# Modulation vectors of two FFN stages: from TensorE matmuls to VectorE products with a sum along the row

## The chip, the cores and the metric

One NeuronCore of a Trainium2 chip runs the whole program. The metric is the device time of one execution in microseconds; for the kernel before there are three timed executions and one more under the hardware profiler.

The engines are named as in the profile: PE is TensorE, DVE VectorE, ACT ScalarE, POOL GpSimd, SP SyncE (here it only issues DMAs).

## The reference, cut to what matters

Two diffusion-transformer blocks follow each other on a latent sequence of 512 tokens and a context of 256 tokens, model width 1024. The first block has two layers (layers 0 and 1 below), the second has one (layer 2). Every layer takes its shifts, scales and gates from an adaLN modulation: the condition vector through SiLU, times a 1024 x 6144 matrix, plus a bias. This is done for two conditions, the latent's and the context's.

```python
def adaln(cond, w_mod, b_mod):
    m = jnp.dot(jax.nn.silu(cond), w_mod) + b_mod
    return jnp.split(m[..., None, :], 6, axis=-1)

sh1, sc1, g1, sh2, sc2, g2 = adaln(c, w_mod[l], b_mod[l])
csh1, csc1, cg1, csh2, csc2, cg2 = adaln(c_ctx, w_mod[l], b_mod[l])
...
x = x + g1 * jnp.einsum('blm,md->bld', mix, w_out[l])
x = x + g2 * swiglu(modulate(rms_norm(x, norm2_g[l]), sh2, sc2), w_ffn_in[l], w_ffn_out[l])
```

## The kernel before

**Arithmetic.** Every large product is computed in three fp32r matmuls: weight and activation are each split into a rounded high part and a rest (`whi`/`wlo`, `hh`/`hl`), and high x high, low x high and high x low are summed in PSUM (`mm3`, L255, L258, L259). The splitting of weights is done on the chip, in `Weights._load`: SP loads half a weight tile (512 KB) into a tile `raw` (L226), ACT casts it into `whi` in two pieces (L229), POOL subtracts to get `wlo` (L231). The split tiles have two buffers, `raw` has four.

**Modulation.** The three layers' modulation is cut into 72 slots of 256 columns, (l, s) in the list `mods`. A slot's weights (1 MB, two `raw` tiles, L218) come from the same four `raw` buffers as the other weights, but are not split. `mod_slot` (L335 to L365) multiplies them in plain fp32 on TensorE: eight calls of a 32 x 256 result (L344; 16 instructions in the trace), the k chunks spread over the four row groups of one PSUM tile. ACT copies that to `ev` (L350), two transposes put columns on partitions (L355), DVE adds the four row groups (`TENSOR_REDUCE`, L357), adds the bias (L359), and for scale slots applies the norm's gain (L363).

**Where the slots run.** `mod_fill` takes slots off the list. 28 of them run at the start and in the mixing stages, where the code puts them between other work. The other 44 are called by `ffn`, one in each step j of layers 0 and 1 (`mod_fill` at L961, 22 steps each). The first four of them are layer 0's own FFN gate, which its first down projection reads (L895); the others are read in layers 1 and 2.

**The FFN.** In `ffn` a step j takes 128 hidden columns: 16 matmul positions of `mm3` over gate and up halves for the latent (tile `s2t`, 512 columns) and, in layer 0 only, as many for the context (`pj`, 256 columns). Then ACT takes SiLU of the gate (`sg`, L955), DVE multiplies by the up half out of PSUM (L956), ACT and POOL split the result (`gh` L327, `gl` L328). After a group of steps (four in layer 0, eight in layer 1, shorter ones at the end) the down projection reads the group's `gh`/`gl`; DVE adds its results into `xt` (`flush`, L895).

**Before the FFN** stands the output projection (`out_proj`), whose last halves run interleaved with the norm of the first halves: DVE and ACT apply it (`u` L423, `hh` L426, `hl` L431 on DVE or L429 on POOL), the row's root goes DVE `rsv` (L297), POOL `rsy` (L298), and a PE broadcast (L323).

**Order.** The program is written in Python order and a list scheduler fixes each engine's static instruction order before the run. Each engine runs its own list in order; semaphores hold an instruction until its inputs have been written and its output buffer is free. Also SP's DMA issues are one such list.

Of the kernel before, what the change touches and what calls it, by code (L numbers as in the profile page):

```python
# [18 lines left out]
D = 1024  # L19
# [20 lines left out]
def _ktile(w):  # L40
    k, n = w.shape
    return np.ascontiguousarray(w.reshape(k // 128, 128, n).transpose(1, 0, 2)).reshape(128, -1)
# [64 lines left out]
    }  # L107


def layout(inp):  # L110
    a = {k: np.asarray(v) for k, v in inp.items()}
    kc = _shape_constants()
    o = {}
# [3 lines left out]
    pv = {  # L117
        "c": a["c"], "c_ctx": a["c_ctx"], "c_2": a["c_2"], "c_ctx_2": a["c_ctx_2"],
        "b_mod0": a["b_mod"][0], "b_mod1": a["b_mod"][1], "b_mod2": a["b_mod_2"][0],
        "n1g0": a["norm1_g"][0], "n1g1": a["norm1_g"][1], "n1g2": a["g_norm_mix_2"][0],  # L120
        "n2g0": a["norm2_g"][0], "n2g1": a["norm2_g"][1], "n2g2": a["g_norm_ffn_2"][0],
        "ghn": a["g_hgrn_norm_2"][0], "gq": a["g_q_norm_2"][0], "gkv": a["g_kv_norm_2"][0],
        "lbf": a["lb_fwd_2"], "lbb": a["lb_bwd_2"], "gfin": a["g_final_2"],
    }
# [20 lines left out]
        o[n] = kc[n]  # L145
    wm = [a["w_mod"][0], a["w_mod"][1], a["w_mod_2"][0]]
    for l in range(3):
        o[f"w_mod{l}"] = np.stack([_ktile(wm[l][:, s * 256:(s + 1) * 256]) for s in range(24)])
    pw = np.zeros((2, 128, 2, 128), np.float32)
    for l in range(2):  # L150
        for ct in range(2):
# [91 lines left out]
class K:  # L243
# [87 lines left out]
    def cond(self, *names):  # L331
        for i, n in enumerate(names):
            self.nc.scalar.activation(out=self.cond_t[:, :, i], in_=self.pv(n), func=AF.Silu)

    def mod_slot(self, l, s, tag="pj"):  # L335

        nc = self.nc
        if (l, s) == (2, 0):
            self.cond("c_2", "c_ctx_2")
        raw = [r.rearrange("p (k n) -> p k n", k=4) for r in self.WM.next(("mod", l, s))]  # L340
        ps = self.ps([128, 256], tag)
        for k in range(KD):
            g = 32 * (k % 4)
            nc.tensor.matmul(ps[g:g + 32], lhsT=self.cond_t[:, k, :], rhs=raw[k // 4][:, k % 4, :],  # L344
                             start=k < 4, stop=k >= 4, tile_position=(0, g))

        ev = self.tmp("ev", [128, 256])

        def post():
            nc.scalar.copy(out=ev, in_=ps)  # L350

        def post2():
            pt = self.ps([128, 2, 128], tag)
            for i in range(2):
# [3 lines left out]
            bc = lambda ap: ap.unsqueeze(2).to_broadcast([128, 2, 2])
            nc.vector.tensor_tensor(out=m, in0=m, in1=bc(self.pv(f"b_mod{l}", 2 * s, 2)), op=ALU.add)  # L359
            q = s // 4  # L360
            if q in (1, 4):
                g = bc(self.pv(f"n{1 if q == 1 else 2}g{l}", 2 * (s % 4), 2))
                nc.vector.scalar_tensor_tensor(out=m, in0=m, scalar=1.0, in1=g, op0=ALU.add, op1=ALU.mult)  # L363
# [1199 lines left out]
    def run(self):  # L1563
# [22 lines left out]
        self.GS = [con.tile([128, 1], F32, name=f"gs{l}") for l in range(2)]  # L1586
        self.cond("c", "c_ctx")
        self.W = Weights(self, self.plan())
        self.mods = [(l, s) for l in range(3) for s in (0, 4, 1, 5, 2, 6, 3, 7) + tuple(range(8, 24))]
        self.WM = Weights(self, [(("mod", l, s), "mod", I[f"w_mod{l}"][s], 2048) for l, s in self.mods])  # L1590
        xs = [[p_dram.tile([128, KD * 256], F32, name=f"xs{l}{i}") for i in range(2)] for l in range(2)]
        v3 = lambda ap: ap.rearrange("p (k n) -> p k n", k=KD)
# [49 lines left out]
        with self.pool("u0") as self.p_u:  # L1642
            h2c, h2 = self.new_h("c"), self.new_h("x")
            self.out_proj(0, self.out_weights(0, 2, 3), hm, hmc, xt, xc, norms(0, 2, xt, h2, xc, h2c))
            self.hc, self.hx = self.new_h("c"), self.new_h("x")
            with self.pool("f0", bufs=8) as pf:
                self.ffn(0, pf, h2, h2c, xt, xc, norms(1, 1, xt, self.hx, xc, self.hc))
            store_xt(xs[0], xt)
        xpool.close()
# [4 lines left out]
        with self.pool("u1") as self.p_u:  # L1654
            h2 = self.new_h("x")
            self.out_proj(1, self.out_weights(1, 2, 3), hm, None, xt, None, norms(1, 2, xt, h2))
            self.hc, self.hx = self.new_h("c"), self.new_h("x")
            with self.pool("f1", bufs=13) as pf:
                xc2 = self.load_x(pf, "xc2", v3(I["c2T"]), NCX, 1)
                self.ffn(1, pf, h2, None, xt, None, norms(2, 1, xt, self.hx), {13: lambda: self.norm_mod(2, 1, xc2, 1, self.hc)})  # L1660
            store_xt(xs[1], xt)
# [99 lines left out]
```

## Time and profile before

| | |
|---|---|
| median of three runs | 2635.28 us (2625.0 to 2635.9) |
| profiled execution | 2631.17 us |
| its span in the trace | 2629.3 us |
| TensorE busy | 2488.1 us, 95% |
| VectorE busy | 966.3 us, 37% |
| ScalarE busy | 909.7 us, 35% |
| GpSimd busy | 1138.1 us, 43% |
| mean granted TensorE clock | 0.971 |

The span runs from the first to the last instruction in the trace; the execution's own time is 1.9 us longer. A busy share is an average over all stages; the stages that this change touches are the two FFNs, from about 450 to 1005 us and from about 1380 to 1770 us.

### The profile page before, as it was taken

To read this page: it belongs to the slowest core of one execution; us is meant where nothing else is said; L and a number is where in the kernel's file an instruction comes from. 1 tells how busy PE (TensorE), PEld (TensorE's weight loads), DVE (VectorE), ACT (ScalarE), POOL (GpSimd) and SP (SyncE) were. 2 spreads that over 40 slices of the span, in tenths; PEclk is the share of its full clock that TensorE was granted. 3 is DMA by queue.
4 is the path that set the end of the run, shared out by engine and by line. 5 is a ranking of instruction groups with operands and counts; after the bars stand their busy time and mean duration, and the time that the engine had idled before them with its cause. 6 is when DMAs were issued, how large, how long until landed. Compare 5 with 4: busy or idle time off the path is not lost.

```text
span 2629.3 us, 38620 instructions
## 1 busy us (share of the span) xinstructions
PE 2488.1 (95%) x15840; PEld 2121.3 (81%) x15840; DVE 966.3 (37%) x1897; ACT 909.7 (35%) x1909; POOL 1138.1 (43%) x960
## 2 busy tenths in 40 slices
PE   7889889999999999989999999999998899999998
PEld 5778779888888889877788777778887788888887
DVE  4897564122121114497542102123322756210113
ACT  4334444312112114333534223234443543422222
POOL 4655305333334335545326445444323354555553
PEclk9889989999999999989999999999998899999999
DMA  7113311323223233122324444343101021232221
GB/s 255 49 50 121 119 57 49 113 96 111 93 86 120 89 97 113 53 64 81 97 81 148 157 129 161 128 153 105 49 33 51 16 97 49 81 96 96 92 91 59
DMA packets 68978, 248.55 MB, mean 95 GB/s; under 512 B 7489, under 2 KB 10817, under 8 KB 67137
## 3 DMA queue, kind: packets, MB, share of 16 engines
q1 hardware_dynamic: 65568, 232.29, 27.1%
q10 hardware_dynamic: 3232, 13.79, 1.4%
q8 instruction: 125, 2.05, 0.3%
q14 instruction: 53, 0.43, 0.1%
HBM read 239.75 MB, written 6.29 MB: 94 GB/s over the span
## 4 chain that ended last, share of the span: by engine, by line
PE 48%; DVE 5%; ACT 2%; POOL 2%; DMA 1%; issue 1%; POOLq 0%; ACTq 0%; DVEq 0%; SPq 0%
PE s2t L255 6%; PE s2t L258 6%; PE s2t L259 6%; PE pj L255 5%; PE pj L258 5%; PE pj L259 5%; PE ap L820 2%; PE ap L259 1%; PE ap L258 1%; PE ap L255 1%; PE s2t L1533 1%; PE s2t L837 1%; DVE mix L665 1%; POOL wlo L231 1%; PE ap L344 1%; PE ap L816 1%
## 5 line engine op out<-in xcount | busy, mean ns | idle before, releaser
L231 POOL TENSOR_TENSOR wlo<-raw,whi 128x512 fp32r<-128x512 f32 x564 | 734.4, 1332 | 683.1 <-ACT whi L229 682.9
L229 ACT CAST whi<-raw 128x512 fp32r<-128x512 f32 x576 | 319.9, 616 | 681.5 <-PE pj L258 252.6
L258 PE MATMUL s2t<-hl,whi 128*128 128x512 f32 (+1 forms) x1184 | 445.6, 377 | 2.6 <-POOL hl L429 2.6
L255 PE MATMUL s2t<-hh,whi 128*128 128x512 f32 (+1 forms) x1184 | 446.9, 379 | 0.9 <-ACT whi L229 0.9
L259 PE MATMUL s2t<-hh,wlo 128*128 128x512 f32 (+1 forms) x1184 | 446.1, 377 | 0.0
L255 PE MATMUL pj<-hh,whi 128*128 128x256 f32 (+1 forms) x1088 | 337.3, 312 | 7.6 <-DVE mod L357 3.0
L258 PE MATMUL pj<-hl,whi 128*128 128x256 f32 (+1 forms) x1088 | 331.2, 305 | 3.3 <-DVE hl L431 2.3
L259 PE MATMUL pj<-hh,wlo 128*128 128x256 f32 (+1 forms) x1088 | 330.6, 305 | 0.0
L956 DVE TENSOR_TENSOR sg<-sg,s2t 128x512 f32<-128x512 f32 x66 | 45.4, 688 | 623.8 <-ACT sg L955 623.8
L258 PEld LDWEIGHTS s2t<-hl,whi 128*128 128x128 f32 x1184 | 222.7, 188 | 46.9 <-POOL hl L429 3.5
L255 PEld LDWEIGHTS s2t<-hh,whi 128*128 128x128 f32 x1184 | 222.3, 188 | 46.7 <-issue 1.6
L259 PEld LDWEIGHTS s2t<-hh,wlo 128*128 128x128 f32 x1184 | 222.7, 188 | 45.5 <-issue 0.8
L255 PEld LDWEIGHTS pj<-hh,whi 128*128 128x128 f32 x1088 | 211.0, 194 | 25.1 <-DVE mod L357 3.3
L328 POOL TENSOR_TENSOR gl<-sg,gh 128x512 fp32r<-128x512 f32 (+1 forms) x66 | 97.2, 1472 | 300.8 <-ACT gh L327 300.8
L258 PEld LDWEIGHTS pj<-hl,whi 128*128 128x128 f32 x1088 | 210.8, 194 | 12.5 <-DVE hl L431 2.5
L259 PEld LDWEIGHTS pj<-hh,wlo 128*128 128x128 f32 x1088 | 210.2, 193 | 8.7 <-issue 0.8
L255 PE MATMUL pj<-whi,hh 128*128 128x256 f32 x672 | 196.8, 293 | 2.5 <-ACT ev L350 1.3
L258 PE MATMUL pj<-wlo,hh 128*128 128x256 f32 x672 | 196.1, 292 | 0.0
L259 PE MATMUL pj<-whi,hl 128*128 128x256 f32 x672 | 194.9, 290 | 0.0
L895 DVE SCALAR_TENSOR_TENSOR xt<-pj,mod,xt 128x256 f32<-128x256 f32 x224 | 101.6, 480 | 174.4 <-PE pj L259 174.2
L955 ACT ACTIVATE sg<-s2t 128x512 f32<-128x512 f32 x66 | 39.2, 594 | 306.4 <-PE s2t L259 306.4
L259 PE MATMUL pj<-gh,wlo 128*128 128x512 f32 (+1 forms) x400 | 145.2, 363 | 0.0
(385 smaller groups left out, 4581.0 us busy)
## 6 DMA issues: line engine op xcount, KB each, us to landing
raw<-in_w_mod SPq DMA_DIRECT2D x144, 512.0 KB, 4.0
raw<-in_w_up SPq DMA_DIRECT2D x132, 512.0 KB, 4.0
raw<-in_w_dn SPq DMA_DIRECT2D x66, 512.0 KB, 3.9
raw<-in_w_in SPq DMA_DIRECT2D x60, 512.0 KB, 3.9
raw<-in_w_out SPq DMA_DIRECT2D x24, 512.0 KB, 3.8
xt<-xs ACTq DMA_DIRECT2D x4, 1024.0 KB, 4.9
xt<-in_xT ACTq DMA_DIRECT2D x2, 1024.0 KB, 8.8
xs<-xt SPq DMA_DIRECT2D x2, 1024.0 KB, 3.8
```

Of the source, the lines that this page charges most:

```text
L229: nc.scalar.copy(out=h, in_=raw[:, q])
L231: eng.tensor_tensor(out=lo[:, s][:, q], in0=raw[:, q], in1=h.bitcast(F32), op=ALU.subtract)
L255: i = mm(ps, lhsT=lh, rhs=rh, start=start, stop=False)
L258: mm(ps, lhsT=lh, rhs=rl, start=False, stop=False)
L259: return mm(ps, lhsT=ll, rhs=rh, start=False, stop=stop)
L328: (lo_eng or self.nc.vector).tensor_tensor(out=lo, in0=src, in1=hi.bitcast(F32), op=ALU.subtract)
L344: nc.tensor.matmul(ps[g:g + 32], lhsT=self.cond_t[:, k, :], rhs=raw[k // 4][:, k % 4, :], start=k < 4, stop=k >= 4, tile_position=(0, g))
L665: nc.vector.scalar_tensor_tensor(out=m, in0=u[:, j:j + W], scalar=dw(j), in1=m, op0=ALU.mult, op1=ALU.add)
L820: i = nc.tensor.matmul(o, lhsT=at[:, j], rhs=v[:, j0 + j, :], start=j0 + j == 0, stop=j0 + j == nj - 1)
L895: self.nc.vector.scalar_tensor_tensor(out=x, in0=ps, scalar=col, in1=x, op0=ALU.mult, op1=ALU.add)
L955: nc.scalar.activation(out=sg[:, c], in_=p[:, 0], func=AF.Silu)
L956: nc.vector.tensor_tensor(out=sg[:, c], in0=sg[:, c], in1=p[:, 1], op=ALU.mult)
```

## The change

For the 44 slots of the first two FFNs (`MODS[20:42]` and `MODS[50:72]`) the host lays the weights out transposed: a partition holds one modulation column, with its 1024 weights along the row; a slot is two such tiles of 128 columns. The function `cond_rows`, called once ahead of each of these FFNs, loads both condition vectors repeated on all partitions (1 MB, `cr`) and applies SiLU on ACT. `mod_rows` takes the place of the matmuls: for each of the two tiles and each of the two conditions, one DVE instruction multiplies the tile by the condition row and writes the row's sum through `accum_out`. The products themselves go to a tile `mjunk`, and for the second condition in place over `raw`. `mod_bias` adds the bias and applies the gain as before. To make room, the FFN pools have 6 buffers where they had 8 (layer 0) and 10 where they had 13 (layer 1). The other 28 slots stay as they were.

```diff
+def _nrows(w):
+
+    return np.ascontiguousarray(w.T.reshape(2, 128, D).transpose(1, 0, 2).reshape(128, 2 * D))
...
+MODS_ROWS = set(MODS[20:42] + MODS[50:72])
...
+    def cond_rows(self, pool, n):
+
+        self.CR = pool.tile([128, 2, D], F32, name="cr", bufs=1)
+        self.junk = pool.tile([128, D], F32, name="mjunk", bufs=1)
+        self.nc.scalar.dma_start(out=self.CR.rearrange("p c k -> p (c k)"), in_=self.I["cr"][n])
+        for i in range(2):
+            self.nc.scalar.activation(out=self.CR[:, i], in_=self.CR[:, i], func=AF.Silu)
+
+    def mod_rows(self, l, s):
+
+        nc = self.nc
+        raw = self.WM.next(("mod", l, s))
+        m = self.MOD[l][:, 2 * s:2 * s + 2, :]
+        acc = self.p_small.tile([128, 2, 2], F32, tag="macc", name="macc", bufs=2)
+
+        def part(i):
+            for ci in range(2):
+                nc.vector.scalar_tensor_tensor(out=raw[i] if ci else self.junk, in0=raw[i], scalar=1.0, in1=self.CR[:, ci],
+                                               op0=ALU.mult, op1=ALU.mult, accum_out=acc[:, i, ci:ci + 1])
+
+        return [(0, lambda: part(0)), (1, lambda: part(1)), (0, lambda: self.mod_bias(l, s, m, acc))]
...
     def mod_slot(self, l, s, tag="pj"):
 
         nc = self.nc
+        if (l, s) in MODS_ROWS:
+            return self.mod_rows(l, s)
...
-            with self.pool("f0", bufs=8) as pf:
+            with self.pool("f0", bufs=6) as pf:
+                self.cond_rows(pf, 0)
                 self.ffn(0, pf, h2, h2c, xt, xc, norms(1, 1, xt, self.hx, xc, self.hc))
...
-            with self.pool("f1", bufs=13) as pf:
+            with self.pool("f1", bufs=10) as pf:
+                self.cond_rows(pf, 1)
```

The change moves instructions at three places that matter below. Line numbers shift with it: L956 becomes L997, L359 L373, L363 L377, L218 L231, L226 L239, L297 L310, L431 L472; the new products are L365.

**VectorE in the middle of FFN 1.** `sg` is the gate product of a step, `mod_88` the modulation of layer 2, `PV` the biases and gains, `macc` the new row sums. Before, two steps in a row:

```order
L956 TENSOR_TENSOR sg<-sg,s2t 128x512 [waits Activation_49]
L357 TENSOR_REDUCE mod_88<-ap 128x4 [waits PE_49]
L359 TENSOR_TENSOR mod_88<-mod_88,PV 128x4 [waits DVE_49]
L956 TENSOR_TENSOR sg<-sg,s2t 128x512 [waits Activation_49]
L357 TENSOR_REDUCE mod_88<-ap 128x4 [waits PE_49]
L359 TENSOR_TENSOR mod_88<-mod_88,PV 128x4 [waits DVE_49]
L363 SCALAR_TENSOR_TENSOR mod_88<-mod_88,PV 128x4 [waits DVE_49]
```

With the change, one step:

```order
L997 TENSOR_TENSOR sg<-sg,s2t 128x512 [waits Activation_49]
L365 SCALAR_TENSOR_TENSOR mjunk,macc<-raw,cr 128x1024 [waits DMAHW3_49]
L365 SCALAR_TENSOR_TENSOR raw,macc<-raw,cr 128x1024 [waits DMAHW5_49,DVE_49,Pool_49]
L365 SCALAR_TENSOR_TENSOR mjunk,macc<-raw,cr 128x1024 [waits DMAHW4_49]
L365 SCALAR_TENSOR_TENSOR raw,macc<-raw,cr 128x1024 [waits DMAHW6_49,DVE_49,Pool_49]
L373 TENSOR_TENSOR mod_88<-macc,PV 128x4 [waits DVE_49]
L997 TENSOR_TENSOR sg<-sg,s2t 128x512 [waits Activation_49]
```

The reduce over PE's result is gone, and between two gate products stand four long products that wait for the slot's weights (a DMA) and for nothing of PE. In the first group of eight steps the products run two slots ahead of the steps, and between the last two gate products of that group there is none.

**SyncE's DMA issues in FFN 1.** Weights of the up projection (`in_w_up`) and of the modulation (`in_w_mod`) take turns in the four `raw` buffers. Before:

```order
L226 DMA raw<-in_w_up 128x1024 [waits DMAHW1_49,PE_49]
L226 DMA raw<-in_w_up 128x1024 [waits DMAHW2_49,PE_49]
L218 DMA raw<-in_w_mod 128x1024 [waits DMAHW7_49,Pool_49]
L218 DMA raw<-in_w_mod 128x1024 [waits DMAHW0_49,Pool_49]
L226 DMA raw<-in_w_up 128x1024 [waits DMAHW5_49,PE_49]
L226 DMA raw<-in_w_up 128x1024 [waits DMAHW6_49,PE_49]
```

With the change:

```order
L239 DMA raw<-in_w_up 128x1024 [waits DVE_49] x2
L231 DMA raw<-in_w_mod 128x1024 [waits DMAHW1_49,Pool_49]
L231 DMA raw<-in_w_mod 128x1024 [waits DMAHW2_49,Pool_49]
L239 DMA raw<-in_w_up 128x1024 [waits DVE_49] x2
L231 DMA raw<-in_w_mod 128x1024 [waits DMAHW5_49,DMAHW3_49,Pool_49]
```

The order of the loads is the same; the up weights' buffers are now given free by VectorE's products, where TensorE's slot gave them free before.

**VectorE at the start of FFN 0.** `u` and `hl` apply the norm to the first latent half (`xt_3680`) and then to the second (`xt_3682`), and `rsv` begins the second half's root. Before:

```order
L423 SCALAR_TENSOR_TENSOR u<-xt_3680,mod_86,ap 128x256 [waits DVE_49]
L431 SCALAR_TENSOR_TENSOR hl<-u,mod_86,hh 128x256 [waits Activation_49] x2
L297 TENSOR_SCALAR rsv<-ap 128x1 [waits PE_49] x2
L956 TENSOR_TENSOR sg<-sg,pj 128x256 [waits Activation_49]
L423 SCALAR_TENSOR_TENSOR u<-xt_3682,mod_86,ap 128x256 [waits DVE_49,PE_49]
```

With the change:

```order
L464 SCALAR_TENSOR_TENSOR u<-xt_3680,mod_86,ap 128x256 [waits DVE_49]
L365 SCALAR_TENSOR_TENSOR mjunk,macc<-raw,cr 128x1024 [waits DMAHW3_49]
L472 SCALAR_TENSOR_TENSOR hl<-u,mod_86,hh 128x256 [waits Activation_49]
L365 SCALAR_TENSOR_TENSOR raw,macc<-raw,cr 128x1024 [waits DMAHW7_49,DVE_49,Pool_49]
L472 SCALAR_TENSOR_TENSOR hl<-u,mod_86,hh 128x256 [waits Activation_49]
L310 TENSOR_SCALAR rsv<-ap 128x1 [waits PE_49]
L365 SCALAR_TENSOR_TENSOR mjunk,macc<-raw,cr 128x1024 [waits DMAHW4_49]
L310 TENSOR_SCALAR rsv<-ap 128x1 [waits PE_49]
L365 SCALAR_TENSOR_TENSOR raw,macc<-raw,cr 128x1024 [waits DMAHW0_49,DMAHW6_49,DVE_49,Pool_49]
L373 TENSOR_TENSOR mod_86<-macc,PV 128x4 [waits DVE_49]
L997 TENSOR_TENSOR sg<-sg,pj 128x256 [waits Activation_49]
```

Three products, two of which wait for a DMA of their own, now stand ahead of the second `rsv`.

## Rows read from the trace of the kernel before

**Rows 1.** The page, parts 1 and 2: busy time of TensorE, and its granted clock.
```profile
PE 2488.1 (95%) x15840; PEld 2121.3 (81%) x15840; DVE 966.3 (37%) x1897; ACT 909.7 (35%) x1909; POOL 1138.1 (43%) x960
...
PEclk9889989999999999989999999999998899999999
```

**Rows 2.** Windows view, the two FFNs: length, engines, granted clock, DMA share, GB/s.
```profile
413.00:1010.00 597.00, 596.05 (x3828) 513.98 (x3828) 122.04 (x279) 145.34 (x282) 223.29 (x178) 1.00 0.30 98
1340.00:1770.00 430.00, 422.27 (x2337) 337.73 (x2335) 83.23 (x189) 138.88 (x271) 219.10 (x183) 1.00 0.43 140
```

**Rows 3.** Timeline of TensorE around one slot in FFN 1 (start us, us, engine, instruction).
```profile
1447.77 0.39 PE L258 MATMUL s2t<-hl,whi 128*128 128x512 f32 x1
1448.00 0.40 PE L259 MATMUL s2t<-hh,wlo 128*128 128x512 f32 x1
1448.33 1.07 PE L344 MATMUL ap<-raw,cond 128*32 128x256 f32 x16
1449.33 0.44 PE L355 MATMUL ap<-ident,ev 128*128 128x128 f32 x2
...
1449.84 0.40 PE L258 MATMUL s2t<-hl,whi 128*128 128x512 f32 x1
```

**Rows 4.** Timeline of VectorE: the gate products of two following steps, FFN 0, FFN 1.
```profile
506.60 0.69 DVE L956 TENSOR_TENSOR sg<-sg,s2t 128x512 f32<-128x512 f32 x1 [10.93 <-ACT sg L955]
...
524.87 0.69 DVE L956 TENSOR_TENSOR sg<-sg,s2t 128x512 f32<-128x512 f32 x1 [10.93 <-ACT sg L955]
...
1461.70 0.69 DVE L956 TENSOR_TENSOR sg<-sg,s2t 128x512 f32<-128x512 f32 x1 [11.32 <-ACT sg L955]
...
1474.27 0.69 DVE L956 TENSOR_TENSOR sg<-sg,s2t 128x512 f32<-128x512 f32 x1 [11.52 <-ACT sg L955]
```

**Rows 5.** Source view, VectorE's products and a scan; ScalarE's group of accumulator reads.
```profile
L423 DVE SCALAR_TENSOR_TENSOR u<-xt,mod,ap x80: 466/476/482, 445.0 to 2253.8; 128x256 f32<-128x256 f32 x80
...
L665 DVE SCALAR_TENSOR_TENSOR mix<-uc,DWH,mix x120: 722/1020/2107, 79.8 to 1200.2; 128x783 f32<-128x783 f32 x60, 128x512 f32<-128x512 f32 x60
...
L845 DVE SCALAR_TENSOR_TENSOR e<-e,rr x40: 458/1010/1462, 127.8 to 1325.8; 128x768 f32<-128x768 f32 x32, 128x256 f32<-128x256 f32 x8
...
L1249 DVE TENSOR_TENSOR_SCAN b<-rst,sig x4: 1757/1758/1759, 2033.4 to 2149.2; 128x768 f32<-128x768 f32 x4
...
L804 ACT ACTIVATION_READ_ACCUMULATOR e<-s2t,nmx 128x1 f32 x96 | 19.2, 200 | 0.0
```

**Rows 6.** Timelines of VectorE and GpSimd in the mixing stage, both busy.
```profile
142.50 3.18 DVE L665 SCALAR_TENSOR_TENSOR mix<-uc,DWH,mix 128x783 f32<-128x783 f32 x2
...
145.68 1.97 DVE L665 SCALAR_TENSOR_TENSOR mix<-uc,DWH,mix 128x783 f32<-128x783 f32 x1
...
139.60 7.21 POOL L231 TENSOR_TENSOR wlo<-raw,whi 128x512 fp32r<-128x512 f32 x4 [12.67 <-ACT whi L229]
```

**Rows 7.** Timelines of FFN 1, one step: ScalarE, GpSimd, TensorE.
```profile
1467.03 2.33 ACT L229 CAST whi<-raw 128x512 fp32r<-128x512 f32 x4 [3.99 <-DMA raw<-in_w_up]
...
1463.12 1.29 POOL L328 TENSOR_TENSOR gl<-sg,gh 128x512 fp32r<-128x512 f32 x1 [2.97 <-ACT gh L327]
1467.73 5.04 POOL L231 TENSOR_TENSOR wlo<-raw,whi 128x512 fp32r<-128x512 f32 x4 [3.33 <-ACT whi L229]
...
1474.67 0.48 PE L255 MATMUL s2t<-hh,whi 128*128 128x512 f32 x1
```

**Rows 8.** TensorE in layer 1's output projection (timeline), and a window in layer 0's.
```profile
1357.41 0.58 PE L255 MATMUL s<-hh,whi 128*128 128x256 f32 x1 [4.34 <-ACT whi L229]
...
412.70:425.00 12.30, 12.30 (x81) 0.77 0.34 111
```

**Rows 9.** Timelines at the start of FFN 0: VectorE, GpSimd, TensorE.
```profile
455.03 0.38 DVE L297 TENSOR_SCALAR rsv<-ap 128x1 f32<-128x1 f32 x2
...
457.80 0.69 POOL L298 TENSOR_TENSOR rsy<-rsv,mhalf 128x2 f32<-128x2 f32 x1
...
460.29 0.38 PE L323 MATMUL ap<-ident,rsy 128*128 128x128 f32 x2
```

More of the change, by code (lines that the diff above doesn't have):

```diff
@@ L107, in _shape_constants @@
     }
+def _nrows(w):
+    return np.ascontiguousarray(w.T.reshape(2, 128, D).transpose(1, 0, 2).reshape(128, 2 * D))
+MODS = [(l, s) for l in range(3) for s in (0, 4, 1, 5, 2, 6, 3, 7) + tuple(range(8, 24))]
+MODS_ROWS = set(MODS[20:42] + MODS[50:72])
 def layout(inp):
@@ L147, in layout @@
     for l in range(3):
-        o[f"w_mod{l}"] = np.stack([_ktile(wm[l][:, s * 256:(s + 1) * 256]) for s in range(24)])
+        o[f"w_mod{l}"] = np.stack([_nrows(wm[l][:, s * 256:(s + 1) * 256]) if (l, s) in MODS_ROWS else _ktile(wm[l][:, s * 256:(s + 1) * 256])
+                                   for s in range(24)])
+    cr = [np.stack([a[n].reshape(-1) for n in p]).reshape(1, -1) for p in (("c", "c_ctx"), ("c_2", "c_ctx_2"))]
+    o["cr"] = np.ascontiguousarray(np.stack([np.broadcast_to(r, (128, 2 * D)) for r in cr]).astype(np.float32))
     pw = np.zeros((2, 128, 2, 128), np.float32)
@@ L333, in cond, with mod_bias @@
             self.nc.scalar.activation(out=self.cond_t[:, :, i], in_=self.pv(n), func=AF.Silu)
+    def cond_rows(self, pool, n):
[14 more added lines that the diff above has]
+        return [(0, lambda: part(0)), (1, lambda: part(1)), (0, lambda: self.mod_bias(l, s, m, acc))]
+    def mod_bias(self, l, s, m, acc):
+        nc = self.nc
+        bc = lambda ap: ap.unsqueeze(2).to_broadcast([128, 2, 2])
+        nc.vector.tensor_tensor(out=m, in0=acc, in1=bc(self.pv(f"b_mod{l}", 2 * s, 2)), op=ALU.add)
+        q = s // 4
+        if q in (1, 4):
+            g = bc(self.pv(f"n{1 if q == 1 else 2}g{l}", 2 * (s % 4), 2))
+            nc.vector.scalar_tensor_tensor(out=m, in0=m, scalar=1.0, in1=g, op0=ALU.add, op1=ALU.mult)
     def mod_slot(self, l, s, tag="pj"):
         nc = self.nc
+        if (l, s) in MODS_ROWS:
+            return self.mod_rows(l, s)
         if (l, s) == (2, 0):
@@ L357, in post2 @@
             nc.vector.tensor_reduce(out=m, in_=pt.rearrange("p c (j r) -> p c r j", j=4)[:, :, 0:2, :], axis=AX.X, op=ALU.add)
[L358 to L363, printed above, removed]
+            self.mod_bias(l, s, m, m)
         return [(0, post), (1, post2)]
@@ L1588, in run @@
         self.W = Weights(self, self.plan())
-        self.mods = [(l, s) for l in range(3) for s in (0, 4, 1, 5, 2, 6, 3, 7) + tuple(range(8, 24))]
+        self.mods = list(MODS)
         self.WM = Weights(self, [(("mod", l, s), "mod", I[f"w_mod{l}"][s], 2048) for l, s in self.mods])
@@ L1734 @@
 INPUTS = (
-    ["xT", "cT", "c2T", "pv", "rb", "k_rope1", "k_rope2", "k_ident", "k_tri", "poolw", "w_kpe", "w_lora", "w_in0", "w_in1", "w_in2"]
+    ["xT", "cT", "c2T", "cr", "pv", "rb", "k_rope1", "k_rope2", "k_ident", "k_tri", "poolw", "w_kpe", "w_lora", "w_in0", "w_in1", "w_in2"]
     + [f"{n}{l}" for n in ("w_mod", "w_out", "w_up", "w_dn") for l in range(3)]
```

## The prediction

> **What bounds the kernel now.** I read the page first. TensorE is busy 95% of the span, and its granted clock is at 0.9 or 1.0 of full speed in nearly every slice [rows 1]. That is an average, so the two FFNs, where the change acts, were read by the windows view: 596.05 us of matmul work in 597 us of FFN 0 with the end of the projection before it, 422.27 in 430 us of FFN 1 with its own, both at clock 1.00, the upper of the two levels (2.4 GHz) [rows 2]. There the time is TensorE's work and little else: what leaves its list shortens the stage, as long as nobody else becomes late. VectorE is busy only 122.04 and 83.23 us in the same windows [rows 2], so there is room for the work that comes.
>
> **What a slot costs TensorE.** Ordinary matmuls start every 0.23 us (1447.77, 1448.00). With a slot between, the second matmul after it starts at 1449.84, 1.84 us after the last one before it; two ordinary steps would have taken 0.47 us [rows 3]. So a slot holds TensorE for 1.84 - 0.47 = 1.37 us: the 16 small matmuls, two transposes, and slower starts on both sides. The step between two gate products is 18.27 us in FFN 0 (506.60 to 524.87) and 12.57 us in FFN 1 (1461.70 to 1474.27) [rows 4], so without slots they would be 16.90 and 11.20 us. 44 slots x 1.37 = **60.3 us**.
>
> **What it costs VectorE.** A product of two SBUF sources takes 476 ns at 256 columns and 1010 ns at 768 [rows 5]: 1.043 ns a column, so 1277 ns at 1024. The sum along the row is what no VectorE row shows. The nearest rows are ScalarE's accumulator read, a separate 200 ns, and VectorE's running sum of two sources, the scan, with 1758 ns at 768 columns [rows 5], which is 2.34 us at 1024. Bounds for one product: 1.28 us if the sum is free, 2.34 if it runs like a scan. I take 1.4, nearer the low end: the instruction is the same as in the product rows, no later column needs an earlier result in its output as in a scan, and for the read of the sum I add 0.1, between nothing and ScalarE's 0.2. Four products and the bias are then 5.8 us a slot, 255 us over 44, and with the gate product (0.69) 6.5 us of a step of 11.20. That is hidden.
>
> The Trainium skill, Vector Engine (DVE) Microarchitecture Reference, section 7 (Points that are easy to get wrong), says of this instruction form that two SBUF sources that aren't bf16 halve its throughput, because both read ports are taken and none is left for the accumulator. The fp32 products above lie between 722 ns at 512 columns (the least of their line) and 1010 at 768, on one line with 476 at 256, or close to it, and show no halving, but none of them accumulates. By that rule a product would be an estimated 2.55 us, and the sum would be near that of the second rival instead of mine.
>
> **GpSimd against VectorE.** In the mixing stage, four subtractions for `wlo` take 7.21 us beside VectorE's two-source products [rows 6], where four alone take 5.04 [rows 7]: speed 0.70. The products take 3.18 for two and 1.97 for one [rows 6], where one of 783 columns alone takes 0.476 + 527 x 0.00104 = 1.02 [rows 5]: speed about 0.6. So the two together get 1.3 times what strict turns would give. A step of FFN 1 has four subtractions and one `gl`, 5.04 + 1.29 = 6.33 us [rows 7], and now 4 x 1.28 = 5.11 us of products: 11.44 us in strict turns, 11.44 / 1.3 = 8.8 us at the speeds seen. Both bounds matter: 8.8 fits in 11.20, 11.44 does not quite. I take the measured sharing. FFN 0 has room either way (16.90).
>
> **Waits that change hands.** SyncE's up loads now wait for VectorE's products instead of TensorE's slot. A pair of `raw` buffers carries in turn a slot and an up tile. A transfer lands 3.99 us after ScalarE begins to wait for it, the first cast takes a quarter of 2.33, the subtractions 5.04 [rows 7]. A whole turn is about 4.0 + 5.6 (products) + 4.0 + 0.6 + 5.0 = 19.2 us, even when the two halves of a pair don't overlap, against two steps, 22.4 us. So the loads keep up, with 3 us over. Today the subtractions end at 1472.77 and TensorE begins the next step at 1474.67 [rows 7]: 1.9 us of slack, of which the shorter step would take 1.37. But that load left only after TensorE's slot; as the products run about two slots ahead of their step, the next load leaves earlier, and the wait left is for TensorE to free `whi`. The gate product behind four products is at most 5.8 us late, which costs nothing inside a group (the `gl` is read only at its end), and in front of the first down projection of FFN 1 no product stands between the last two gate products.
>
> **The starts.** At the start of FFN 0 `rsv` runs at 455.03, GpSimd's root at 457.80, TensorE's broadcast of it at 460.29 [rows 9]. Now three products, two with a transfer of their own to wait for, stand ahead of the second `rsv`. TensorE has matmuls of the first step to do meanwhile; bounds 0 (all covered) and 8 us (three products at 1.4 plus a transfer of 4) for each FFN. I take 2 each, since the root's chain had about 5 us from `rsv` to broadcast and most of the matmuls of the first half come ahead of it. The 1 MB condition rows and two SiLU of some 1.1 us come while ScalarE waits in the output projection. On the other side, the first slot's products free `raw` buffers early, for which the projection's own weights now wait: TensorE stands 4.34 us for ScalarE's cast of them in layer 1 [rows 8], and the clock after a like stall in layer 0 was 0.77 [rows 8]. Bounds of that gain: 0 and 10 us in both layers together; I take 3, near the low end, because in layer 1 the two SiLU stand ahead of the cast that TensorE waits for.
>
> The 44 copies that leave ScalarE, the 44 reduces that leave VectorE and the fewer FFN buffers (six for groups of four, ten for groups of eight) I cost at nothing: what hides them is TensorE's list, full in both stages [rows 2].
>
> **Sum.** Profiled execution 2631.2 - 60.3 + 4 - 3 = **2572 us**. The execution lies 4.1 us under the median of the three runs (2635.28). A measurement of this kernel can tell some 0.5%, 13 us, from no change.
>
> **Rivals.**
> (a) *GpSimd and VectorE share badly in FFN 1.* With strict turns and accumulator reads of 0.2 each (4 x 0.2 on 11.44) a step takes 12.2 instead of 11.20, and only 0.3 of 1.37 us is won in each of 22 steps. FFN 0 still gives 30. Together 2631 - 30 - 7 = 2594, or, if the load turn of 19.2 us grows past 22.4 instead by the stretched times, about the same. For it: four subtractions at 7.21. Against: the joint speed of 1.3.
> (b) *The sum runs at the scan's rate, and the two engines take strict turns.* Then a step of FFN 1 needs 4 x 2.34 + 6.33 = 15.7 us against today's 12.57: 3.1 lost in each of 22 steps, 69 us. FFN 0, at 16.90, holds 15.7 and still wins 30; the starts, with longer products ahead of the norm, lose 8. 2631 + 69 - 30 + 8 = 2678, **slower**. It decides in FFN 1's steady steps, once four products and 6.33 pass 12.57, from 1.56 us a product on in strict turns, and the whole kernel loses from about 1.9. With a joint speed of 1.3 the same products would give 12.1 a step and a time near 2600. Against it: the product rows. For it: no row has the sum.
> (c) *The starts cost more.* The products ahead of `rsv` wait for their transfers 6 us longer in each FFN, and TensorE comes back at the lower clock as it does after the stalls in the projections [rows 8]: 15 us more, 2587.
> (d) *The slot was filling TensorE's wait for weights*, so that its time turns into a wait for `wlo`: the 1.9 us of slack says that only if the loads don't leave earlier; then only 0.3 a step is won in both FFNs, 2631 - 44 x 0.3 = 2618.
>
> **How the numbers follow.** My forecast 0.66, (a) 0.12, (b) 0.09, (c) 0.08, (d) 0.05. The forecast's own range is 2561 (no cost at the starts, 10 won in the projections) to 2587 (16 lost at the starts, nothing won); one of the three runs lies 6 us under the profiled execution, which takes the low end to 2555. With (c) and (a), whose worst is FFN 1's 30 all lost, 2602, the range is 2555 to 2602; (b), (d) and the edges lie outside. Faster by over 0.5%: forecast, (a), (c) and half of (d), less a little for what I overlooked: 0.85. Within 0.5%: the other half of (d) and part of (b): 0.07. Slower: 0.08.
>
> **What would show it.** Right: FFN windows shorter by 30 us each with TensorE still busy over 98% of them, gate products 11.2 and 16.9 us apart, products of 1.3 to 1.5 us alone, VectorE busy some 240 us more. (a) or (b) would show as TensorE waits for `wlo` in every step of FFN 1, with products over 1.9 us for (b); (c) as waits near 460 and 1385 us. The forecast is wrong if TensorE waits for weights in the steady steps.

## The result, and the profile after

The changed kernel takes 2596.0 us, the median of four runs (2591.14 to 2603.19), where the kernel before takes 2635.11 (four runs); ratio 0.9863 with a 95% interval of 0.9828 to 0.9897. That is 39 us faster, some 60% of the 63 between forecast and median. The time lies inside the range, on the spot of rival (a), but not by that rival's mechanism: it has TensorE wait for `wlo` in every step of FFN 1, and the profile shows two such waits, both at FFN 1's start (from 1380 to 1400 us), and in the steps five for the gate product.

The page after: the lines that answer to [rows 1].

```profile
PE 2436.6 (94%) x15048; PEld 2125.5 (82%) x15048; DVE 1220.4 (47%) x2205; ACT 890.8 (34%) x1869; POOL 1189.6 (46%) x960
...
PEclk9889989999999999989989999999998899999999
```

TensorE is 51.5 us less busy (2488.1 before), VectorE 254.1 more (966.3 before). Windows of the changed kernel (columns as in [rows 2]): FFN 0, layer 1's projection, FFN 1.

```profile
470.00:1010.00 540.00, 535.59 (x3202) 477.75 (x3202) 213.01 (x393) 121.69 (x231) 218.74 (x161) 1.00 0.32 102
1340.00:1360.00 20.00, 13.52 (x63) 12.63 (x64) 9.61 (x16) 7.88 (x13) 10.50 (x9) 0.53 0.44 140
1400.00:1750.00 350.00, 339.09 (x1549) 280.34 (x1547) 184.82 (x272) 99.92 (x186) 214.91 (x149) 1.00 0.48 152
```

FFN 0 is full still. In FFN 1 TensorE now stands 10.9 of 350 us, and in layer 1's projection it is busy 13.52 of 20 us at a mean granted clock of 0.53, nearly the lower of its two levels (before, the two slices of 10 us around the same wait, from 1350 to 1370 us, had 0.85 and 0.98). What TensorE waited for from 1300 to 1770 us (total, times, longest):

```profile
PE s L268 <- ACT whi L242: 8.6, 2, 7.1
PE ap L336 <- POOL rsy L311: 6.7, 2, 3.4
PE s2t L268 <- DVE sg L997: 4.9, 5, 1.7
PE s L268 <- DVE xt L936: 2.7, 1, 2.7
PE s2t L272 <- POOL wlo L244: 2.5, 2, 1.2
```

So the gain of the slots is there, and it is given back at two places: around FFN 1's start, and in FFN 1's steps.

**The products.** The new instructions by line 365 (least, median and greatest ns):

```profile
L365 DVE SCALAR_TENSOR_TENSOR mjunk<-raw,cr x88: 1212/1225/2407, 397.2 to 1729.0; 128x1024 f32<-128x1024 f32 x88
L365 DVE DVE_READ_ACCUMULATOR mjunk<-raw,cr x88: 75/80/84, 398.3 to 1730.2; 128x1 f32 x88
L365 DVE SCALAR_TENSOR_TENSOR raw<-raw,cr x88: 1209/1226/2326, 398.7 to 1730.3; 128x1024 f32<-128x1024 f32 x88
```

A product alone takes 1225 ns, and the read of its sum is an instruction of its own, 80 ns: 1.3 us, at the low end of [rows 5].

**FFN 1's steps** became 12.4 us and more, not 11.2. One of them, with the next two gate products, on the queues of SyncE, ScalarE, GpSimd, VectorE and TensorE:

```profile
1432.15 0.80 SPq L239 DMA_DIRECT2D raw<-in_w_up  x2
1435.05 0.80 SPq L231 DMA_DIRECT2D raw<-in_w_mod  x2
1442.88 3.89 SPq L239 DMA_DIRECT2D raw<-in_w_up  x2
1446.88 0.84 SPq L231 DMA_DIRECT2D raw<-in_w_mod  x2
...
1438.51 0.59 ACT L996 ACTIVATE sg<-s2t 128x512 f32<-128x512 f32 x1
...
1436.93 7.06 POOL L244 TENSOR_TENSOR wlo<-raw,whi 128x512 fp32r<-128x512 f32 x4 [0.77 <-ACT whi L242]
...
1439.39 1.22 DVE L365 SCALAR_TENSOR_TENSOR mjunk<-raw,cr 128x1024 f32<-128x1024 f32 x1 [3.21 <-DMA raw<-in_w_mod]
...
1440.66 2.19 DVE L365 SCALAR_TENSOR_TENSOR raw<-raw,cr 128x1024 f32<-128x1024 f32 x1
...
1442.78 2.30 DVE L365 SCALAR_TENSOR_TENSOR mjunk<-raw,cr 128x1024 f32<-128x1024 f32 x1
...
1445.18 1.23 DVE L365 SCALAR_TENSOR_TENSOR raw<-raw,cr 128x1024 f32<-128x1024 f32 x1
...
1446.72 0.68 DVE L997 TENSOR_TENSOR sg<-sg,s2t 128x512 f32<-128x512 f32 x1
...
1459.07 0.68 DVE L997 TENSOR_TENSOR sg<-sg,s2t 128x512 f32<-128x512 f32 x1
...
1471.42 0.68 DVE L997 TENSOR_TENSOR sg<-sg,s2t 128x512 f32<-128x512 f32 x1
...
1447.45 0.50 PE L268 MATMUL s2t<-hh,whi 128*128 128x512 f32 x1 [1.68 <-DVE sg L997]
```

Read it as a loop. The slot's two loads leave at 1435.05, when the last product of the slot before is done with its buffer; in the next turns they stand in SyncE's list behind an up load that waits for that product. The first lands at 1439.39. The four products, two of them stretched to 2.2 and 2.3 us by GpSimd's subtractions (7.06 us for four instead of 5.04), end at 1446.4. Only then does VectorE come to the gate product, whose SiLU ScalarE began at 1438.51; TensorE had stood 1.68 us for it, because the gate product also frees one of the two PSUM tiles `s2t`. And only then do the second up load and, behind it, the next slot's loads leave (1446.88). The turn is 1446.88 - 1435.05 = 11.8 us here, and 12.55 and 12.35 in the next two (slot loads at 1459.43 and 1471.78).

**Layer 1's projection and FFN 1's start:**

```profile
1332.29 0.34 ACTq L352 DMA_DIRECT2D cr<-in_cr  x1
1332.66 0.46 ACTq L1601 DMA_DIRECT2D xc<-in_c2T  x1
...
1332.90 2.97 SPq L239 DMA_DIRECT2D raw<-in_w_out  x2
...
1341.55 1.14 ACT L242 CAST whi<-raw 128x512 fp32r<-128x512 f32 x2 [8.91 <-DMA raw<-in_w_out]
...
1344.00 2.00 ACT L354 ACTIVATE cr<-cr 128x1024 f32<-128x1024 f32 x2
...
1342.22 0.58 PE L268 MATMUL s<-hh,whi 128*128 128x256 f32 x1 [7.15 <-ACT whi L242]
...
1345.09 1.22 DVE L365 SCALAR_TENSOR_TENSOR mjunk<-raw,cr 128x1024 f32<-128x1024 f32 x1 [11.93 <-ACT cr L354]
...
1352.18 0.48 DVE L936 SCALAR_TENSOR_TENSOR xt<-s,mod,xt 128x256 f32<-128x256 f32 x1
...
1352.72 0.58 PE L268 MATMUL s<-hh,whi 128*128 128x256 f32 x1 [2.66 <-DVE xt L936]
```

Two transfers of 1 MB leave ahead of the projection's last weights; the one of `cr` is new. The first of the weights lands 8.6 us after its issue (1332.90 to 1341.55). TensorE stands 7.15 us for it (4.34 before, [rows 8]). Then four products wait for the SiLU of the condition rows, run for 7 us, and hold back the `xt` flushes behind them: 2.66 us more for TensorE, at the low clock. Behind the projection TensorE waits for GpSimd's root as well, 3.3 us from 1380 to 1400 us (0.4 before); the other such wait in the list, 3.4 us, comes in FFN 1's steps.

### The profile page after: what moved, and what is told of

Read it like the earlier page. It is cut to its first block, busy times and chain, and to the rows that moved or that the text cites. A ratio compares the mean times of both kernels' runs of the same rounds, so it can differ in the third digit from the quotient of the medians.

```text
span 2601.4 us, 37319 instructions
## 1 busy us (share of the span) xinstructions
PE 2436.6 (94%) x15048; PEld 2125.5 (82%) x15048; DVE 1220.4 (47%) x2205; ACT 890.8 (34%) x1869; POOL 1189.6 (46%) x960
## 5 line engine op out<-in xcount | busy, mean ns | idle before, releaser
L244 POOL TENSOR_TENSOR wlo<-raw,whi 128x512 fp32r<-128x512 f32 x564 | 777.5, 1409 | 814.8 <-ACT whi L242 814.5
L997 DVE TENSOR_TENSOR sg<-sg,s2t 128x512 f32<-128x512 f32 x66 | 45.1, 683 | 349.6 <-ACT sg L996 349.6
L365 DVE SCALAR_TENSOR_TENSOR mjunk<-raw,cr 128x1024 f32<-128x1024 f32 x88 | 128.1, 1456 | 168.0 <-DMA raw<-in_w_mod 155.9
L271 PE MATMUL pj<-gl,whi 128*128 128x512 f32 (+1 forms) x400 | 144.2, 361 | 0.0
L268 PE MATMUL pj<-gh,whi 128*128 128x512 f32 (+1 forms) x400 | 144.2, 361 | 0.0
```

Source lines behind the costliest of these rows:

```text
L244: eng.tensor_tensor(out=lo[:, s][:, q], in0=raw[:, q], in1=h.bitcast(F32), op=ALU.subtract)
L268: i = mm(ps, lhsT=lh, rhs=rh, start=start, stop=False)
L271: mm(ps, lhsT=lh, rhs=rl, start=False, stop=False)
L365: nc.vector.scalar_tensor_tensor(out=raw[i] if ci else self.junk, in0=raw[i], scalar=1.0, in1=self.CR[:, ci], op0=ALU.mult, op1=ALU.mult, ...
L997: nc.vector.tensor_tensor(out=sg[:, c], in0=sg[:, c], in1=p[:, 1], op=ALU.mult)
```

## The experiments

Twelve kernels ran, in three groups of four, each group on one chip with its own runs of before. "Step" is the distance of gate products in FFN 1.

**1, 2. Before and after again, one chip**

> The kernel before, unchanged, for a second profile of it on the chip of the next three runs. All theories: gate products of FFN 1 12.2 to 12.6 us apart. In the first profile of before the 512-column matmuls start every 233 ns, in that of the changed kernel every 227 ns. If that pace belongs to the chip or the moment, this profile has one pace in common with the next one; if it belongs to the change, this one shows 233 and the next 227.

> The changed kernel, unchanged, on the same chip. All theories: 0.983 to 0.990 of before. Theory 1 (a loop in FFN 1: the slot's transfer waits in SyncE's list behind an up load that waits for the last slot's products, and the next gate product waits on VectorE behind the products of that transfer): gate products of FFN 1 some 12.3 us apart, with TensorE waiting 1.2 to 1.7 us for a gate product in the steps of the first group, and the broadcasts at both FFN starts late by 5 to 10 us against before. Rival 2 (VectorE and GpSimd taking turns at SBUF are the bound by themselves): TensorE waits for wlo instead.

Before took 2638.67 us (one run; median of its group's seven runs of before 2632.96); after 2596.45, ratio 0.9859 [0.9836, 0.9883]. Steps are 12.57 and some 12.4 us; TensorE waits for gate products, as theory 1 has it. The pace belongs to the kernel, not to the chip. Layer 2's FFN, whose instructions are the same in both, before and then after:

```profile
2400.00 0.39 PE L258 MATMUL s2t<-hl,whi 128*128 128x512 f32 x1
...
2400.69 0.40 PE L258 MATMUL s2t<-hl,whi 128*128 128x512 f32 x1
```

```profile
2399.96 0.39 PE L268 MATMUL s2t<-hh,whi 128*128 128x512 f32 x1
...
2400.64 0.39 PE L268 MATMUL s2t<-hh,whi 128*128 128x512 f32 x1
```

Three matmuls on in each case. Over longer stretches it is every 233 ns there and every 227 here, both at clock 1.00, in FFN 0 as in layer 2's FFN. 256-column matmuls differ the other way: 117.8 against 119.9 ns in the first 300 us, 118.8 against 120.0 in FFN 0 (medians over rows of twelve).

**3. FFN 0 alone**

```diff
-MODS_ROWS = set(MODS[20:42] + MODS[50:72])
+MODS_ROWS = set(MODS[20:42])
...
-            with self.pool("f1", bufs=10) as pf:
-                self.cond_rows(pf, 1)
+            with self.pool("f1", bufs=13) as pf:
```

FFN 1's pool and its condition rows are as before too.

> Only FFN 0's 22 slots as products; FFN 1 and its start as before. Theory 1: FFN 0 wins 30 us less some 7 at its start, 23 in all, 0.991; that is more than half of what the whole change wins, since FFN 1 with its start wins the rest, about 16, by 30 minus start and loop. Rival 2 says the same of FFN 0 (16.9 us steps hold both engines). If FFN 1 with its start gave nothing, this would be as fast as the whole change (0.986).

2600.63 us, ratio 0.9885 [0.9858, 0.9911]: some 30 us against before, where 23 were expected; the faster pace of run 2 is in it. The intervals of this and of the whole change overlap, so moving FFN 1's 22 slots was worth some 7 us, not clear of nothing. The timelines of the two say where it went: from FFN 1's second gate product to its last run 2 takes 332.1 us where this takes 349.1, 17.0 won, and from the last flush of the first half of layer 1's projection to that second gate product it takes 85.7 where this takes 67.7, 18.0 lost.

**4. Products behind their step's gate product, and own buffers for the slots**

```diff
-                    nc.vector.tensor_tensor(out=sg[:, c], in0=sg[:, c], in1=p[:, 1], op=ALU.mult)
+                    self.sg_ins = nc.vector.tensor_tensor(out=sg[:, c], in0=sg[:, c], in1=p[:, 1], op=ALU.mult)
...
+        own = self.sg_ins
...
+                self.order(t, own)
...
+                raw = k.p_mraw.tile([128, hn], F32, tag="mraw", name="mraw", bufs=2) if own else k.p_raw.tile([128, hn], F32, tag="raw", name="raw")
```

> The whole change, with two edits: the products of a step's slot may not run before that step's own gate product, and the slots' weights have two buffers of their own, so that up loads wait for GpSimd alone. The FFN pools shrink to 5 and 8 buffers for them. Theory 1: the loop of FFN 1 is cut and no product stands in the norm at the starts: steps of 10.9 to 11.2 us, TensorE not waiting for gate products, starts within 3 us of before, 0.977 to 0.981 of before. Rival 2: sharing of SBUF is as before, so steps stay above 12 us with waits for wlo, and only the starts win: 0.983 to 0.986.

2593.63 us, 0.9849 [0.9825, 0.9873], short of what theory 1 expected, but its steps did what it says. FFN 1 of this kernel on VectorE:

```profile
1562.23 0.69 DVE L1002 TENSOR_TENSOR sg<-sg,s2t 128x512 f32<-128x512 f32 x1 [2.07 <-ACT sg L1001]
1562.83 2.27 DVE L369 SCALAR_TENSOR_TENSOR mjunk<-mraw,cr 128x1024 f32<-128x1024 f32 x1
...
1565.15 2.19 DVE L369 SCALAR_TENSOR_TENSOR mraw<-mraw,cr 128x1024 f32<-128x1024 f32 x1
...
1567.27 2.29 DVE L369 SCALAR_TENSOR_TENSOR mjunk<-mraw,cr 128x1024 f32<-128x1024 f32 x1
...
1569.61 1.23 DVE L369 SCALAR_TENSOR_TENSOR mraw<-mraw,cr 128x1024 f32<-128x1024 f32 x1
...
1573.11 0.69 DVE L1002 TENSOR_TENSOR sg<-sg,s2t 128x512 f32<-128x512 f32 x1 [2.07 <-ACT sg L1001]
```

Three of four products are still stretched to 2.2 us by GpSimd, and yet gate products come 10.88 us apart and nothing of TensorE waits for them: sharing alone does not bound the step. From the second gate product of FFN 1 to its last this kernel won 35.0 us against run 1. But TensorE still waited 7.2 us for the cast in layer 1's projection, where the condition rows still load, so the starts were not all cured. And FFN 0 lost half its gain: TensorE waited 9.6 us for `gl` at its down projections. Run 7, with 6 buffers there, no buffers of the slots' own and only its first two slots held, shows 1.9 us of that wait; which of the three differences makes it was not separated.

**5, 6. The pace**

```diff
+        t = self.p_small.tile([128, 2, 2], F32, tag="macc", name="macc", bufs=2)
+        nc.vector.memset(t, 0.0)
         self.p_hx = es.enter_context(tc.tile_pool(name="hx", bufs=KD))
```

> The kernel before with one unused tile of 2 x 16 bytes a partition in the pool of small tiles, as the row sums take there in the change, so that all tiles of the pools opened after it (the split activations h among them, TensorE's moving operands) lie 32 bytes further. Theory 3 (part of the time won is TensorE's pace, which hangs on where tiles lie in SBUF, not on the moved work): 512-column matmuls every 227 ns, 256-column ones every 119.7 in place of 233.3 and some 117, and 0.992 to 0.996 of before. If the pace has another cause: 233 ns and 0.998 to 1.002.

2620.9 us, 0.9959 [0.9944, 0.9975], matmuls every 227 ns: 11 us from an unused tile that shifts the later ones. One third of layer 2's 512-column matmuls (count, least, median and greatest ns, first and last start), in run 1 and here:

```profile
L255 PE MATMUL s2t<-hh,whi x107: 393/398/398, 2399.8 to 2474.0; 128*128 128x512 f32 x107
...
L255 PE MATMUL s2t<-hh,whi x88: 389/389/389, 2399.6 to 2458.8; 128*128 128x512 f32 x88
```

That is 74.2 us for 106 x 3 matmuls and 59.2 for 87 x 3. The 256-column matmuls did only half of what was expected: 120.0 ns in the first 300 us, but 118.8 in FFN 0, as before.

```diff
-        acc = self.p_small.tile([128, 2, 2], F32, tag="macc", name="macc", bufs=2)
+        self.p_acc = pool
...
+        acc = self.p_acc.tile([128, 2, 2], F32, tag="macc", name="macc", bufs=2)
```

> The change with the row sums in the FFNs' own pools instead of the pool of small tiles, so that the later tiles lie where they lay before the change. Theory 3: the pace goes back to 233 ns, and the time to 2605 to 2615, 0.990 to 0.994 of before; then some 16 of the 37 us won came from the shift by 32 bytes. If the pace has another cause: 227 ns and 0.984 to 0.988, like the change.

2602.44 us, 0.9892 [0.9872, 0.9913], matmuls every 233 ns, the time a little under what was expected. So of the 37 us that the change won on the chip of runs 1 and 2, some 9 to 11, and not 16, come from where 32 bytes of row sums lie, and the moved work is worth some 28. (The pace is plain in the rows; the split of the time is rough, since the intervals of runs 2 and 6 overlap.) A step of FFN 0 in this kernel:

```profile
674.97 0.69 DVE L998 TENSOR_TENSOR sg<-sg,s2t 128x512 f32<-128x512 f32 x1 [7.25 <-ACT sg L997]
...
691.86 0.69 DVE L998 TENSOR_TENSOR sg<-sg,s2t 128x512 f32<-128x512 f32 x1 [6.29 <-ACT sg L997]
```

**7. All losses taken away**

```diff
-                self.cond_rows(pf, 0)
-                self.cond_rows(pf, 1)
...
+                if l < 2 and j == 0:
+                    self.cond_rows(pf, l, act)
...
+        t = self.nc.scalar.dma_start(out=self.CR.rearrange("p c k -> p (c k)"), in_=self.I["cr"][n])
+        self.order(t, act)
...
+                if (l, s) in MODS[20:22] + MODS[50:72]:
+                    self.order(t, own)
```

`act` is the first step's SiLU. The slots have buffers of their own in FFN 1 alone (its pool at 8, FFN 0's at 6).

> The whole change with the losses taken away one by one: the condition rows are loaded after the first step's SiLU of each FFN (not in the output projection), the first two slots of FFN 0 and all of FFN 1 may not run ahead of their own step's gate product, and in FFN 1 the slots' weights have two buffers of their own (FFN 0's pool keeps 6 buffers, FFN 1's has 8). Theory 1: the starts are as before, FFN 0 wins its 30 and FFN 1 its 30, with the 16 of the pace 2566 to 2576, 0.974 to 0.978 of before. If the starts' loss is not the condition rows and the products in front, it stays at 0.982 or above.

2567.99 us, the median of three executions, 0.9749 [0.9715, 0.9784], some 64 us under its group's before (2631.78), faster than both kernels. (A fourth execution took 8184 us; it isn't in the ratio, and nothing here explains it.) TensorE's longest waits from 1280 to 1760 us, none of which is in a step:

```profile
PE s L269 <- ACT whi L243: 5.4, 2, 4.6
PE ap L337 <- POOL rsy L312: 1.6, 2, 1.0
PE s L269 <- DVE sg L1004: 1.5, 1, 1.5
```

**8. No reads by GpSimd in FFN 1**

```diff
-                eng.tensor_tensor(out=lo[:, s][:, q], in0=raw[:, q], in1=h.bitcast(F32), op=ALU.subtract)
+                if eng is nc.gpsimd and getattr(k, "quiet", False):
+                    nc.gpsimd.memset(lo[:, s][:, q].bitcast(F32), 0.0)
...
+                self.quiet = True
```

> The change with GpSimd's subtractions in FFN 1 left out: it writes zeros into wlo instead, so reads nothing from SBUF there. One look at the steps of FFN 1. Theory 1: the loop is a landing of 4.3 us, four products and a bias; without the stretching by GpSimd the products take 5.2 us instead of some 7, the loop is 10 us, under TensorE's 10.9, so steps fall to 10.9 to 11.2 without waits for gate products. If the loop does not need the sharing, steps stay above 12.

One run, 2577.88 us. The products take 1224 ns (median). From the third to the sixth step of the first group steps are 11.0 to 11.8 us, in the second group 10.88 for the first four, and TensorE waits for no gate product there, with the shared buffers and the order of the change untouched. The loop needs the stretching too: 5.2 us of products fit, 7 do not. This edit also frees `raw` sooner, since GpSimd no longer reads it; in the turns shown above that was not the wait that ended last, since there the loads wait for VectorE's products.

**9. The condition rows later, and nothing else**

```diff
-                self.cond_rows(pf, 1)
...
+                if l < 2 and j == 0:
+                    self.cond_rows(pf, l, act)
```

> The change with one edit: the condition rows of each FFN are loaded and put through SiLU behind the SiLU of its first step, so no product can stand in the norm before it and no 1 MB transfer beside the output projection's weights. Theory 1: the starts come back, some 6 us at FFN 0 and 15 at FFN 1; FFN 1's loop stays, steps of 12 to 12.4 us with waits for gate products: 0.978 to 0.981 of before. If the starts' loss had another cause, 0.985 like the change.

2595.68 us, 0.9853 [0.9831, 0.9875], as the change. The wait for the projection's weights fell to 4.1 us, as before, and from the last flush of the projection's first half to FFN 1's second gate product it took 68.2 us, as with the shift alone (67.5, run 5), where run 2 took 85.7. So what the starts lost hangs on the place of the condition rows. But the products that could not run early then pile up in the first steps: the next two gate products are 24.6 and 19.7 us apart, with one wait of 7.7 us for `whi`, and from the second gate product to the last it took 346.4 us instead of 332.1. Most of what was won at the start went into the loop.

**10, 11. The two halves of run 4, in FFN 1 alone**

```diff
+                if (l, s) in MODS[50:72]:
+                    self.order(t, own)
```

> The change with one edit: in FFN 1 no product of a slot may run before its own step's gate product (the raw buffers stay shared with the up weights). Theory 1: gate products no longer stand behind products that wait for a transfer, but the up loads then wait for products that run later, so the loop changes form: TensorE waits for wlo or whi instead, steps between 11.2 and 12.4, 0.980 to 0.986. If the place of the products alone makes the loop, steps fall to 10.9 to 11.2 as with the own buffers.

2609.05 us, 0.99 [0.9881, 0.9919], slower than expected, and slower than the change where the edit acts: 358.2 us from FFN 1's second gate product to its last, against 332.1 in run 2. Steps are 12.7 us, longer than expected too, and TensorE waits for split weights instead (1400 to 1600 us):

```profile
PE s2t L272 <- POOL wlo L244: 6.4, 10, 1.4
PE s2t L268 <- ACT whi L242: 2.5, 3, 1.2
```

```diff
+        self.p_mraw = pool if n == 1 else None
...
-            with self.pool("f1", bufs=10) as pf:
+            with self.pool("f1", bufs=8) as pf:
```

> The change with one edit: in FFN 1 the slots' weights have two buffers of their own (its pool shrinks to 8). Theory 1: up loads no longer wait for products, so the loop is cut and steps are 10.9 to 11.3; but the products run still further ahead, eight slots of them in the norm at FFN 1's start, which costs 20 to 40 us there: 0.984 to 0.995. If the sharing of buffers is not part of the loop, steps stay at 12 to 12.4.

2621.46 us, 0.995 [0.9932, 0.9968]. The second group's steps are 10.88 us, so the shared buffers are the other half of the loop; but the first group's are 14 to 17, and from the last flush of the projection's first half to FFN 1's second gate product it takes 99.0 us, 13 more than in run 2, since more products stand in the norm:

```profile
PE ap L451 <- DVE rsv L311: 4.6, 1, 4.6
PE s L269 <- DVE xt L938: 7.3, 1, 7.3
```

**12. A shift of 64 bytes**

```diff
+        t = self.p_small.tile([128, 2, 4], F32, tag="macc", name="macc", bufs=2)
```

> The kernel before with an unused tile twice as large, so that the later tiles lie 64 bytes further instead of 32. One look at the pace: if it hangs on where a tile begins within 64 bytes, it is 233 ns again as without the tile; if on any shift, 227.

One run, 2619.34 us, 227 ns again: so it is not a tile's place within 64 bytes that decides. Which boundary sets the pace stays open.

## Why the prediction was right or wrong

The sum of the forecast was -59 us against the profiled execution. Where an instruction of a mark starts against before (run 1), in us, from the timelines of runs 1, 2 and 5 to 7 (roots by TensorE's broadcast of them, flushes on VectorE); the last line is the span. Columns by run; runs 5 to 7 ran on another chip than 1 and 2. These are single executions: that of run 1 was 6 us above its group's median, that of run 2 as much below its own; and in layer 1's mixing, where the change moves nothing, run 6 loses 6.4 and run 2 wins 2.6.

| mark | 5: shift alone | 6: work alone | 2: the change | 7: losses away |
|---|---|---|---|---|
| first norm root in layer 0's projection | -1.6 | -7.3 | -4.9 | -2.5 |
| root of the second half, FFN 0's start | -0.9 | -1.4 | +1.6 | -1.7 |
| first norm root after FFN 0 | -4.9 | -34.7 | -34.6 | -31.9 |
| mixing of layer 1, its first root | -4.3 | -35.0 | -34.1 | -31.4 |
| layer 1's projection, last flush of its first half | -7.0 | -28.6 | -36.7 | -28.1 |
| layer 1's projection, last flush | -5.9 | -18.3 | -24.8 | -24.3 |
| second gate product of FFN 1 | -6.7 | -12.2 | -18.2 | -21.8 |
| last gate product of FFN 1 | -13.6 | -33.7 | -40.7 | -61.1 |
| end | -18.2 | -35.4 | -47.9 | -70.6 |

- *A slot holds TensorE for 1.37 us*: right. FFN 0's step went from 18.2 to 16.87 us with the old pace (run 6), 1.3 a slot, so rival (d) fell. From the last flush of layer 0's projection to the first root after FFN 0, its start included, run 6 took 552.4 us where run 1 took 579.9: 27.5 won of 22 x 1.37 = 30.1.
- *A product takes 1.4 us, hidden*: 1.225 and 0.08 alone, up to 2.4 beside GpSimd; VectorE 254 us more, as forecast. Rival (b) fell. The rule of the Trainium skill (Vector Engine (DVE) Microarchitecture Reference, section 7) is not borne out as the prediction applied it (2.55 us a product): fp32 sources and a sum ran at 1.2 ns a column, no halving against the 1.043 without a sum.
- *Measured sharing, 8.8 us of 11.20*: the engines' load was no bound, as run 4 shows with steps of 10.88 us, but the 1.3 was a misreading. Where a product and a subtraction really overlap, they take 2.2 to 2.3 us each instead of 1.225 and 1.26: together 1.225/2.25 + 1.26/2.27, some 1.1 times strict turns, not 1.3. In the 7.21 us of [rows 6] VectorE also ran a reduction out of PSUM, which left the reads of SBUF to GpSimd for a while:

```profile
141.64 0.94 DVE L800 TENSOR_REDUCE nmx<-s2t 128x1 f32<-128x768 f32 x1
```

At 1.1 the 11.44 us would be an estimated 10.4, which still fits. So rival (a) was nearly right on the sharing and wrong that it bounds the step by itself; its second branch, a load turn grown by stretched products, comes nearest to what ran, though with TensorE waiting for the gate product and not for `wlo`. What I left out is that sharing stretches a product that others wait for (run 8).

- *"So the loads keep up, with 3 us over"*: this step failed. I closed the turn over two steps, a pair of buffers each; SyncE's in-order list ties the pairs together, so slot load, products and the issue behind them make a turn of 12 us in every step.
- *"The gate product ... costs nothing inside a group"*: this failed too. I looked for who reads its result, and not at the PSUM tile it frees. It waited 7.6 us behind products that waited for a transfer. The sign that I had named, TensorE waiting for weights in the steady steps, would not have shown it. The two together, from the second to the last gate product of FFN 1, where the forecast had 20 steps x 1.37 = 27 us: the work won 21.5 at the old pace (run 6), and 15.6 to 17.0 at the new one (run 2 against run 5 and against run 3), presumably since a step that waits in the loop does not get the faster pace.
- *"I take 2 each" for the starts, and 3 won in the projections*: failed most, and in layer 1's projection. From the last flush of its first half to its last flush it took 32.7 us in run 1 and 33.8 with the shift, but 43.0 in run 6 and 44.7 in run 2: 10 to 11 lost where my bounds were 0 to 10 won. FFN 1's start behind it, up to the second gate product, lost 6 to 7 more, inside my 8 but not 2. Run 9 brings both back, so they come from the condition rows and the products behind them. FFN 0's start cost nothing: the second half's root came 5.8 us later behind the projection's last flush than before (16.7 against 10.9), yet FFN 0 from that flush to the next root took 549.6 us in run 2 and 550.1 in run 9, where the root came in time. Rival (c) had FFN 1's start and the low clock right, but put the price on the root; most of it lay in the projection, where I had hoped to win. In layer 0's projection the work won 3.3 us (17.0 instead of 20.3 between its halves), the 3 that I had assumed for both layers.
- *The copies, reduces and smaller pools at nothing*: nothing in the runs speaks against the copies and reduces. In FFN 0 TensorE waited 2.8 us for `gl` in the changed kernel and not at all before, about what is missing of the 30.1; whether that comes from 6 buffers or from GpSimd's stretched work no run separates.
- *Not in the sum at all*: the pace, 11 us in run 5. Without it the change takes 2602.4 (run 6), just past the end of my range. That the range held the time was partly this luck. The 2572 comes near a kernel whose loads and starts do not get in the way: run 7 took 2568, some 2579 without the shift's 11.

## What to carry to other kernels

Work moved to an idle engine is hidden only if what stands behind it in that engine's order, and the buffers it holds, can wait; follow a buffer's turn through the in-order DMA queue, not only through the buffers. An early start of such work looks free to a scheduler and costs at the stage's start: hold it behind the first step, and give its loads buffers of their own. Here each of these alone won nothing clear or lost (runs 9 to 11), and all together won 28 us more than the change (run 7). When a change adds even a small tile, compare a stage that it doesn't touch before crediting the change with the time.

## What was not expected of the hardware

- The pace of matmuls hangs on where tiles lie: an unused 32 (or 64) bytes a partition ahead of later pools took 512-column matmuls from 233.3 to 226.7 ns and 256-column ones in the first 300 us from 117.8 to 120.0, at a granted clock of 1.00, for 0.41% of the time (0.25 to 0.56%). Which tile or boundary decides is open.
- VectorE's sum along the row costs next to nothing: 80 ns for its read, and the product itself 1225 ns at 1024 columns, a little less than the 1277 that shorter products promised.
- VectorE's product of two SBUF sources and GpSimd's subtraction all but take turns: 2.2 to 2.3 us each while they overlap, against 1.225 and 1.26 alone. Where GpSimd only writes (run 8), the product keeps its 1.224 us.
